# Layer 0's gated MLP: first projection as seven products of quarters, with weight sums on GpSimd

## The chip, the cores and the metric

One core of a Trainium2 chip runs the kernel. The metric is device time in microseconds (us) of one execution; runs are compared by their medians. Engines are TensorE (PE in the profile, with PEld for its weight loads), VectorE (DVE), ScalarE (ACT), GpSimd (POOL) and SyncE (SP), which issues the loads.

## The reference

A two-layer diffusion block over 512 latent tokens and 256 context tokens (768 together, `LAT` and `CTX`), model width 1024. Layer 0 mixes tokens with gated linear attention (GLA), layer 1 with neighbourhood attention. Behind each mixer stands a gated MLP, with a width-3 convolution along the tokens. With `h` the normalized and modulated input (`x * rms * (1 + scale) + shift`, where scale and shift come from adaLN projections of a condition vector), the MLP is

```python
a, v = jnp.split(h @ w_in, 2, axis=-1)            # 1024 -> 2 x 2816
a = conv3(a) + b                                  # per channel, along tokens; context and latent apart
x = x + gate * ((jax.nn.silu(a) * v) @ w_out)     # 2816 -> 1024
```

## The kernel before

Activations are kept with the channels on the 128 partitions and the tokens on the free axis. A number is split in a high and a low part (`hi`, `lo`); a product is three matmuls, `lo*hi`, `hi*lo`, `hi*hi` (`mm3`). Weights come from memory as 512 KB tiles `st` (128 x 1024, three buffers), issued by SP in order; ACT writes the high part `wh` (L244), DVE the low part `wl` (L245); five buffers hold each of them (`wunit`).

The hidden width 2816 is 22 tiles of 128 channels, in groups of three (the last of four). For each tile j, `in_tile` multiplies two weight tiles, `a` (the one that goes through the convolution) and the value `v`, with the eight channel blocks of `H`, for the 512 latent and the 256 context tokens: 2 x 8 x 3 matmuls of 512 columns and as many of 256. ACT copies the first result into `apad` (L788); DVE does the three taps (L822, L823, L824), ACT the silu (L825), DVE multiplies with the value out of PSUM (L830), and the result is split in `uh` and `ul` (L261, L262). After a group comes its output projection: for each of eight output blocks d, three tiles times LAT and CTX, added to the residual by DVE (`add_gated`, L273). The first two tiles (`in_first`) run over LAT while the normalization of CTX is being finished.

In layer 0's MLP, DVE also computes layer 1's adaLN vectors: `ada_lanes` gives 64 steps, each a 512 KB load `sa` and one multiply-add into `acc` (L203), four after each hidden tile.

Each engine runs its own queue in order. A scheduler decides that order from the dependencies and the buffers in the pools; only the program's own order and the pool sizes are written by hand.

Of the kernel before, what the change touches and what calls it, by code (L numbers as in the profile page):

```python
# [16 lines left out]
KD = 8  # L17
# [22 lines left out]
def body(ctx, tc, x, ctx_x, small, ada0, ada, w_gla, a_w1, a_w2, w_go, w_fi, w_fo,  # L40
# [8 lines left out]
    whl = ctx.enter_context(tc.tile_pool(name="whl", bufs=5))  # L49
# [49 lines left out]
    one0 = cst.tile([128, 32], F32, name="one0")  # L99
    nc.gpsimd.memset(one0, 0.0)  # L100
    nc.gpsimd.memset(one0[:, 0:1], 1.0)

# [61 lines left out]
    def ada_step(l, m, i):  # L164
# [12 lines left out]
        rows = sml.tile([128, 256], F32, name="rows", tag="rows", bufs=1)  # L177
# [10 lines left out]
    ada_jobs = []  # L188

    def ada_lanes(pool, l, m, c):  # L190
# [4 lines left out]
        def step(k):  # L195
            if k == 0:
                acc[0] = pool.tile([128, 1024], F32, name="acc", tag="acc", bufs=1)
# [9 lines left out]
            for j in range(4):  # L207
                mm(ps[32 * j:32 * j + 32, 0:256], one0, acc[0][:, 256 * j:256 * j + 256], start=True, stop=True,
                   skip_group_check=True)
            rows = sml.tile([128, 256], F32, name="rows", tag="rows", bufs=1)  # L210
            nc.scalar.activation(rows, ps[:, 0:256], AF.Copy)
            pm = ps_aux()
            for f in range(2):
                nc.tensor.transpose(pm[:, f * 128:(f + 1) * 128], rows[:, f * 128:(f + 1) * 128], ident)
            o = 8 * m
            mod = modT[l][:, o:o + 8, c]
            bias = sT[:, R_AB + 48 * l + o:R_AB + 48 * l + o + 8]
            nc.vector.tensor_add(mod.rearrange("p (j i) -> p j i", i=2),
                                 pm[:, 0:256].rearrange("p (i j s) -> p j i s", i=2, j=4)[:, :, :, 0],
                                 bias.rearrange("p (j i) -> p j i", i=2))  # L220
# [8 lines left out]

    def wunit(src, eng=None, scales=None):  # L230
# [3 lines left out]
        st = wst.tile([128, n], F32, name="st", tag="st")  # L234
        nc.sync.dma_start(st, src)
        hi = whl.tile([128, n], FR, name="wh", tag="wh")
        lo = whl.tile([128, n], FR, name="wl", tag="wl")
# [10 lines left out]
    def mm3(out, a, b, first, last):  # L248
        mm(out, a[1], b[0], start=first, stop=False)  # L249
        mm(out, a[0], b[1], start=False, stop=False)  # L250
        mm(out, a[0], b[0], start=False, stop=last)  # L251
# [23 lines left out]
    class Norm:  # L275


        def __init__(self, pool, l, n, rng, tag="t2", spread=False, blocks=False):
            self.__dict__.update(pool=pool, l=l, n=n, rng=rng, tag=tag, spread=spread, blocks=blocks)
            self.w = rng[1] - rng[0]  # L280
            self.acc = None

        def tmp(self, name):
            return self.pool.tile([128, 512], F32, name=name, tag=self.tag)[:, 0:self.w]

        def add(self, k):

            if self.acc is None:
                self.acc = self.pool.tile([128, self.w], F32, name="nacc", tag=f"nacc{self.w}", bufs=2)
# [24 lines left out]
        def apply(self, k):  # L314
# [5 lines left out]
            t = self.tmp("hf")  # L320
# [9 lines left out]
            nc.vector.scalar_tensor_tensor(lo, t, b_, hi.bitcast(F32), OP.add, OP.subtract)  # L330

# [38 lines left out]
    with tc.tile_pool(name="gla", bufs=6) as pool:  # L370
# [261 lines left out]
        def part_a(h, extra=None):  # L632
            vr_group(h, 0)
            diag(h)
            for i in range(7):
                level(h, i)
                todo = ada_step(*blocks.pop(0)) if blocks and i < 6 else None
# [93 lines left out]
    def finish_gla(pool):  # L731

        nonlocal X
        X = load_x()
        lat, cx = Norm(pool, 0, 1, LAT), Norm(pool, 0, 1, CTX)
        units = {}
        for d in range(KD):
            w, ps = early[d] if d < 3 else (out_unit(d), ps_mm())
# [16 lines left out]
    def ffn(l, after):  # L755
        first = 0 if l == 0 else 2
        seqs = ((0, 256), (256, 768)) if l == 0 else ((256, 768),)
        rngs = (LAT, CTX) if l == 0 else (LAT,)
        base = seqs[0][0]
        n_tok = 768 - base  # L760
        n_pad = n_tok + len(seqs) + 1

        def pad_of(tok):
            return tok - base + 1 + (1 if len(seqs) == 2 and tok >= 256 else 0)

        with tc.tile_pool(name=f"ffn{l}", bufs=4) as pool:
            left = finish_gla(pool) if l == 0 else []
            apad = [pool.tile([128, n_pad], F32, name=f"apad{i}", tag=f"apad{i}", bufs=1) for i in range(2)]
            edges = [0, n_pad - 1] + ([257] if len(seqs) == 2 else [])
            for ap_ in apad:  # L770
                for e in edges:
                    nc.gpsimd.memset(ap_[:, e:e + 1], 0.0)

            def pieces(a, b):
                return [(max(a, s0), min(b, s1)) for s0, s1 in seqs if max(a, s0) < min(b, s1)]

            def in_weights(j, which):
                return tuple(w.rearrange("p (k n) -> p k n", k=KD) for w in wunit(w_fi[l, j, which]))

            def in_group(j, which, w, rng):  # L780
                a, b = rng
                ps = ps_mm() if which == 0 else ps_aux()
                for k in range(KD):
                    mm3(ps[:, 0:b - a], (w[0][:, k, :], w[1][:, k, :]),
# [418 lines left out]
```

## Time and profile before

| what | value |
|---|---|
| median of three runs | 1739.43 us (1738.65 to 1744.02) |
| profiled execution | 1739.42 us, span 1737.6 us, mean granted clock 0.993 |
| TensorE busy | 1681.7 us, 97% |
| DVE, ACT, GpSimd busy | 1070.4 (62%), 658.7 (38%), 190.9 us (11%) |
| read from memory | 173.75 MB, 101 GB/s over the span |

Stages, in us from the span's start: first normalization and GLA 0 to 385; its output projection and second normalization to about 465; layer 0's MLP about 441 to 1040; neighbourhood attention 1050 to 1370; layer 1's MLP to the end. Rows of the profile give an instruction's start, duration, engine, line, operation, `out<-in` and shape; what stands in brackets is the idle time ahead of it and who ended that. Rows by form give the number of instructions, their busy time, the mean in ns and the idle time before them.

### The profile page before, as it was taken

The numbers are of one execution on the slowest core, as the hardware profiler recorded it, in microseconds if no ns is written. First come the engines' busy times: TensorE is split into PE (matmuls) and PEld (weight loads), VectorE is DVE, ScalarE is ACT, GpSimd is POOL, SyncE is SP. The second block draws the span as 40 slices with busy tenths as digits, with TensorE's granted clock in tenths as the row PEclk, the third lists the DMA queues.
The fourth block names the chain that finished last, engine by engine and source line by source line (L and its number), as shares of the span: only waits on it lengthen the run. The fifth ranks groups of instructions, "written<-read, shape, count | busy, mean of one in ns | idle before, by whom it ended". The sixth has DMA issues, their size and how long they took to land.

```text
span 1737.6 us, 27175 instructions
## 1 busy us (share of the span) xinstructions
PE 1681.7 (97%) x11107; PEld 1413.8 (81%) x11107; DVE 1070.4 (62%) x1699; ACT 658.7 (38%) x1173; POOL 190.9 (11%) x324
## 2 busy tenths in 40 slices
PE   5999999999999999999999999999999999999997
PEld 3767778778888888888888888888888888888887
DVE  4797777977666655656544575445456755555555
ACT  3675655653422121212213264443334522222332
POOL 1031212220000000000000015332222000000000
PEclk9999999999999999999999999999999999999999
DMA  7553423026224543544412122112111233223321
GB/s 274 173 171 122 154 90 104 19 72 220 86 73 152 160 125 110 179 147 146 122 60 86 49 68 79 54 42 66 54 56 42 75 97 98 90 82 95 109 85 49
DMA packets 54188, 179.70 MB, mean 103 GB/s; under 512 B 7024, under 2 KB 10864, under 8 KB 54064
## 3 DMA queue, kind: packets, MB, share of 16 engines
q1 hardware_dynamic: 54064, 177.97, 32.6%
q8 instruction: 87, 1.43, 0.3%
q14 instruction: 37, 0.30, 0.1%
HBM read 173.75 MB, written 2.10 MB: 101 GB/s over the span
## 4 chain that ended last, share of the span: by engine, by line
PE 80%; DVE 10%; ACT 4%; DMA 2%; issue 2%; POOL 1%; SPq 0%; POOLq 0%; DVEq 0%; ACTq 0%
PE mm L249 18%; PE mm L251 17%; PE mm L250 17%; PE aux L249 6%; PE aux L250 6%; PE aux L251 6%; PE mm L1006 2%; DMA sa<-in 2%; PE aux L989 2%; PE aux L964 2%; DVE t L526 1%; PE aux L605 1%; PE aux L570 1%; DVE acc L203 1%; DVE t L525 1%
## 5 line engine op out<-in xcount | busy, mean ns | idle before, releaser
L249 PE MATMUL mm<-hh,wl 128*128 128x512 f32 (+3 forms) x1104 | 388.6, 354 | 3.9 <-ACT hh L329 2.5
L251 PE MATMUL mm<-hh,wh 128*128 128x512 f32 (+3 forms) x1104 | 383.3, 348 | 0.0
L250 PE MATMUL mm<-hl,wh 128*128 128x512 f32 (+3 forms) x1104 | 383.0, 347 | 0.0
L244 ACT ACTIVATE wh<-st 128x1024 fp32r<-128x1024 f32 (+1 forms) x189 | 196.2, 1052 | 314.1 <-PE mm L251 162.4
L245 DVE TENSOR_TENSOR wl<-st,wh 128x1024 fp32r<-128x1024 f32 (+1 forms) x188 | 229.1, 1228 | 32.3 <-ACT wh L244 31.7
L249 PEld LDWEIGHTS mm<-hh,wl 128*128 128x128 f32 (+1 forms) x1104 | 208.8, 190 | 35.8 <-issue 5.5
L250 PEld LDWEIGHTS mm<-hl,wh 128*128 128x128 f32 (+1 forms) x1104 | 209.4, 190 | 24.3 <-issue 0.8
L251 PEld LDWEIGHTS mm<-hh,wh 128*128 128x128 f32 (+1 forms) x1104 | 209.1, 189 | 24.4 <-issue 0.4
L249 PE MATMUL aux<-hh,wl 128*128 128x512 f32 (+2 forms) x576 | 201.1, 349 | 0.0
L250 PE MATMUL aux<-hl,wh 128*128 128x512 f32 (+2 forms) x576 | 201.0, 349 | 0.0
L251 PE MATMUL aux<-hh,wh 128*128 128x512 f32 (+2 forms) x576 | 200.8, 349 | 0.0
L249 PE MATMUL mm<-uh,wl 128*128 128x512 f32 (+1 forms) x560 | 194.1, 350 | 1.7 <-ACT uh L261 1.4
L250 PE MATMUL mm<-ul,wh 128*128 128x512 f32 (+1 forms) x560 | 194.2, 348 | 0.0
L251 PE MATMUL mm<-uh,wh 128*128 128x512 f32 (+1 forms) x560 | 193.3, 346 | 0.0
L273 DVE SCALAR_TENSOR_TENSOR xl<-mm,mod,xl 128x512 f32<-128x512 f32 (+1 forms) x168 | 116.3, 698 | 108.9 <-PE mm L251 108.6
L305 POOL TENSOR_TENSOR rs<-ms,mhalf 128x2 f32<-128x2 f32 (+1 forms) x10 | 11.6, 1160 | 1036.6 <-DVE ms L303 1036.6
L249 PEld LDWEIGHTS mm<-uh,wl 128*128 128x128 f32 x560 | 105.8, 190 | 20.0 <-ACT uh L261 3.7
L249 PEld LDWEIGHTS aux<-hh,wl 128*128 128x128 f32 x576 | 109.2, 190 | 15.0 <-issue 1.4
L250 PEld LDWEIGHTS aux<-hl,wh 128*128 128x128 f32 x576 | 109.2, 190 | 14.4 <-issue 1.1
L251 PEld LDWEIGHTS aux<-hh,wh 128*128 128x128 f32 x576 | 109.1, 189 | 14.0 <-issue 0.8
L250 PEld LDWEIGHTS mm<-ul,wh 128*128 128x128 f32 x560 | 106.4, 190 | 14.3 <-DVE ul L262 0.3
L251 PEld LDWEIGHTS mm<-uh,wh 128*128 128x128 f32 x560 | 106.2, 190 | 13.1
(207 smaller groups left out, 2462.4 us busy)
## 6 DMA issues: line engine op xcount, KB each, us to landing
st<-in SPq DMA_DIRECT2D x201, 512.0 KB, 3.7
sa<-in SPq DMA_DIRECT2D x98, 512.0 KB, 4.3
sx<-in SPq DMA_DIRECT2D x14, 512.0 KB, 5.7
xl<-in SPq DMA_DIRECT2D x8, 512.0 KB, 5.6
xc<-in SPq DMA_DIRECT2D x4, 512.0 KB, 7.8
out<-y SPq DMA_DIRECT2D x16, 128.0 KB, 1.7
raw<-in SPq DMA_DIRECT2D x16, 96.0 KB, 2.4
t<-q SPq DMA_DIRECT2D x16, 64.0 KB, 2.0
```

The source lines that it names most:

```text
L203: nc.vector.scalar_tensor_tensor(acc[0], st, cs[:, k, c:c + 1], acc[0], OP.mult, OP.add)
L244: nc.scalar.activation(hi, st, AF.Copy)
L245: (eng or nc.vector).tensor_sub(lo, st, hi.bitcast(F32))
L249: mm(out, a[1], b[0], start=first, stop=False)
L250: mm(out, a[0], b[1], start=False, stop=False)
L251: mm(out, a[0], b[0], start=False, stop=last)
L273: nc.vector.scalar_tensor_tensor(x_, ps, gate(l, n, d, rng), x_, OP.mult, OP.add)
L525: nc.vector.tensor_mul(eq, eq, st[h]["q"])
L526: nc.vector.tensor_mul(ek, ek, st[h]["k"])
L964: mm(pss[hh][:, off:off + 256], qe[a_][p_, 128 * t:128 * t + 128], ke[b_][p_, ks], start=i == 0, stop=i == 2)
L989: nc.tensor.transpose(pT[:, i * 128:(i + 1) * 128], S2[:, o:o + 128], ident)
L1006: mm(po[64 * hh:64 * hh + 64, 128 * t:128 * t + 128], V[:, vs[i], 64 * hh:64 * hh + 64], PTs[hh][:, i * 128:(i + 1) * 128], start=i == 0, ...
```

## The change

`ffn` is written as `ffn0` and `ffn1`; layer 1's stays as it was. In layer 0, tiles 0 and 1 are computed as before (`plain`). For tiles 2 to 21 the product of the two weight tiles with `H` is seen as a 2 x 2 block product: output halves `a` and `v`, channel halves of four blocks, token halves of 384 columns. Eight quarter products become seven, by sums of weight quarters and of input quarters (the scheme of Strassen and Winograd):

- Input sums, once: GpSimd makes four sums for each of four block pairs out of `R` (the normalized input in full precision, which the normalization now writes as well, with one more ACT instruction a block). They are split into `T2`, `T3`, `T4`; quarter 12 of `H` is overwritten by a sum, the other three stay.
- Weight sums, per tile: GpSimd makes four sums of 128 x 512 in place (L928 to L931). `S1` goes to a buffer of its own, `S3` into the first half of the value tile, `S2` and `S4` into the halves of the first tile. Seven quarters are split by ACT (L237) and DVE (L238): `A` as one 1024-wide unit, the others 512 wide. The split parts go into a ring of ten 512-wide slots, in the order in which TensorE uses them.
- Order on TensorE per tile: `first` (products 11, 21), `middle` (2, 12, 3), `final_` (22, 4), 12 matmuls of 384 columns each; `first` of the next tile stands ahead of `final_` of this one, `middle` of the next behind it. Results are gathered in three PSUM buffers; ACT copies intermediate results out (`cp`, L867, three a tile) and DVE adds them (L948, L949, L959, L964).
- The middle tap of the convolution goes to ACT (L784). There is one `apad` instead of two.
- The output weights of a group come in halves of 512 columns, rearranged on the host beside the other layouts.
- adaLN: two steps a tile instead of four; the running sum takes one of the two `sa` buffers; half of the steps (m = 2 to 5) move into neighbourhood attention, four a pair of heads, of which the scheduler pulls some ahead. The end of a vector is eight matmuls of two columns instead of a product and transposes.

```diff
@@ ada_lanes
-                acc[0] = pool.tile([128, 1024], F32, name="acc", tag="acc", bufs=1)
+                acc[0] = ast.tile([128, 1024], F32, name="acc", tag="sa")
...
+            for d in range(KD):
+                mm(ps[:, 2 * d:2 * d + 2], acc[0][:, d * 128:d * 128 + 128], ones, start=True, stop=True)
@@ weights
+    NW = 10
+    WR = tuple(res.tile([128, NW * 512], FR, name=nm) for nm in ("wh", "wl"))
...
+    def wsplit(st):
+        out, o = [], 0
+        for a, b in wspans(st.shape[-1] // 512):
+            hi, lo = (w[:, a:b] for w in WR)
+            s_ = st[:, o:o + b - a]
+            nc.scalar.activation(hi, s_, AF.Copy)
+            nc.vector.tensor_sub(lo, s_, hi.bitcast(F32))
...
@@ Norm.apply
+            if self.keep:
+                nc.scalar.activation(t, t, AF.Identity, bias=b_)
@@ ffn0
+            def sums(k):
+                a, b = slice(0, HT), slice(HT, T)
+                r, q = R[k], R[k + 4]
+                sub = nc.gpsimd.tensor_sub
+                sub(r[:, a], r[:, b], r[:, a])
+                sub(r[:, b], q[:, b], r[:, b])
+                sub(q[:, b], q[:, b], r[:, a])
+                sub(q[:, a], q[:, a], q[:, b])
+                for i, src in ((2, q[:, b]), (3, r[:, b]), (4, q[:, a])):
+                    split_to(TT[i][0][:, k, :], TT[i][1][:, k, :], src)
...
+            def weights_b(j):
+                s_ = st[j]
+                a, v = s_["a"], wload(w_fi[0, j, 1])
+                s1 = pool.tile([128, 512], F32, name="s1", tag="s1")
+                h = (slice(0, 512), slice(512, 1024))
+                nc.gpsimd.tensor_add(s1, v[:, h[0]], v[:, h[1]])
+                nc.gpsimd.tensor_sub(v[:, h[0]], a[:, h[0]], v[:, h[0]])
+                nc.gpsimd.tensor_sub(a[:, h[0]], s1, a[:, h[0]])
+                nc.gpsimd.tensor_sub(a[:, h[1]], a[:, h[1]], a[:, h[0]])
+                for nm, t_ in (("S2", a[:, h[0]]), ("S1", s1), ("S3", v[:, h[0]])):
+                    s_[nm], = wsplit(t_)
+                s_["left"] = a[:, h[1]], v[:, h[1]]
...
+            def first(j):
+                s_["b1"], s_["b2"] = ps_aux(), ps_mm()
+                product(s_["b1"], s_["A"][0], 11, True)
+                s_["s1"] = copied(s_["b1"])
+                product(s_["b2"], s_["A"][1], 21, True)
...
+            def middle(j):
+                s_["b5"] = ps_aux()
+                product(s_["b1"], s_["S2"], 2, False)
+                s_["u2"] = copied(s_["b1"])
+                product(s_["b5"], s_["S1"], 12, True)
+                product(s_["b1"], s_["S3"], 3, False)
+                s_["u3"] = copied(s_["b1"])
+                nc.vector.tensor_add(s_["u3"], s_["b5"][:, 0:HT], s_["u3"])
+            def final_(j):
+                product(s_["b5"], s_["S4"], 22, False)
+                nc.vector.tensor_add(apad[:, 386:770], s_["b5"][:, 0:HT], s_["u2"])
+                product(s_["b1"], s_["A22"], 4, False)
+                u = finish(j, [(0, 256, b1[:, 0:256]), (256, HT, b1[:, 256:HT]), (HT, T, s_["u3"])])
+                for job in jobs[:2]:
+                    job()
...
+                    if j < NF - 1:
+                        weights_a(j + 1)
+                    weights_c(j)
+                    if j < NF - 1:
+                        first(j + 1)
+                    us[j] = final_(j)
+                    if j < NF - 1:
+                        to_pad(j + 1)
+                        weights_b(j + 1)
+                        middle(j + 1)
@@ neighbourhood attention, four times a pair of heads
+            jobs.pop(0)()
```

DVE in the second group, while a tile's hidden values are finished. Before, tile 4: `tt` is its convolution, `st` a weight tile, `sa` a load for adaLN.

```order
L822 TENSOR_SCALAR tt_5667<-apad0_4765,sT_109 128x769 [waits Activation_49]
L203 SCALAR_TENSOR_TENSOR acc_5679<-sa_5818,cs_115,acc_5679 128x1024 [waits DMAHW1_49,DVE_49]
L823 SCALAR_TENSOR_TENSOR tt_5667<-apad0_4765,sT_109,tt_5667 128x769 [waits DVE_49]
L245 TENSOR_TENSOR wl_5850<-st_5847,wh_5849 128x1024 [waits DMAHW4_49,PE_49,Activation_49]
L824 SCALAR_TENSOR_TENSOR tt_5667<-apad0_4765,sT_109,tt_5667 128x769 [waits DVE_49]
L203 SCALAR_TENSOR_TENSOR acc_5679<-sa_5821,cs_115,acc_5679 128x1024 [waits DMAHW2_49]
L830 TENSOR_TENSOR u_5672<-tt_5667,aux_5617 128x512 [waits PE_49,Activation_49]
L203 SCALAR_TENSOR_TENSOR acc_5679<-sa_5824,cs_115,acc_5679 128x1024 [waits DMAHW3_49,DVE_49]
L830 TENSOR_TENSOR u_5672<-tt_5667,aux_5642 128x256 [waits PE_49]
L245 TENSOR_TENSOR wl_5856<-st_5853,wh_5855 128x1024 [waits DMAHW5_49,Activation_49]
```

After, tiles 3 to 5: `tt_5514` is tile 3's convolution, `st_5589` and `st_5672` are tile 5's two weight tiles, `st_5727` is tile 6's first, and L948, L949 write tile 4's sum to `apad`.

```order
L238 TENSOR_TENSOR wl_121<-st_5589,wh_120 128x512 [waits Activation_49]
L786 SCALAR_TENSOR_TENSOR tt_5514<-apad_4166,sT_103,tt_5514 128x769 [waits DVE_49]
L238 TENSOR_TENSOR wl_121<-st_5672,wh_120 128x512 [waits DMAHW1_49,Activation_49]
L948 TENSOR_TENSOR apad_4166<-mm_5462,cp_5475 128x256 [waits DVE_49]
L949 TENSOR_TENSOR apad_4166<-mm_5462,cp_5475 128x128
L882 TENSOR_TENSOR tt_5514<-tt_5514,aux_5136 128x256 [waits PE_49,Activation_49]
L882 TENSOR_TENSOR tt_5514<-tt_5514,aux_5136 128x128
L882 TENSOR_TENSOR tt_5514<-tt_5514,cp_5262 128x384 [waits DVE_49]
L238 TENSOR_TENSOR wl_121<-st_5727,wh_120 128x1024 [waits DMAHW2_49,Activation_49]
L275 TENSOR_TENSOR ul_5520<-tt_5514,uh_5519 128x768 [waits Activation_49]
L959 TENSOR_TENSOR cp_5586<-aux_5547,cp_5586 128x384 [waits Activation_49]
L238 TENSOR_TENSOR wl_121<-st_5589,wh_120 128x512 [waits PE_49,Activation_49]
```

Between one tile's taps and products now stand the splits of a tile two further on, each behind ACT's high part, and three adds out of PSUM.

ACT at the same place. Before, tiles 4 and 5: `wh` the high parts of weights, `apad` the copies out of PSUM.

```order
L788 ACTIVATE apad0_4765<-mm_5559 128x512 [waits PE_49]
L788 ACTIVATE apad0_4765<-mm_5585 128x256 [waits PE_49]
L244 ACTIVATE wh_5849<-st_5847 128x1024 [waits DMAHW4_49,Activation_49]
L825 ACTIVATE tt_5667<-tt_5667 128x769 [waits DVE_49]
L244 ACTIVATE wh_5855<-st_5853 128x1024 [waits DMAHW5_49,PE_49,Activation_49]
L261 ACTIVATE uh_5675<-u_5672 128x768 [waits DVE_49]
L788 ACTIVATE apad1_4766<-mm_5698 128x512 [waits PE_49,Activation_49]
L788 ACTIVATE apad1_4766<-mm_5724 128x256 [waits PE_49,Activation_49]
```

After: `cp_5475`, `cp_5560` and `cp_5586` are tile 4's three copies, and the splits in between are of tile 5's sums (`s1_5674`, `st_5589`, `st_5672`) and of tile 6's first tile.

```order
L867 ACTIVATE cp_5475<-aux_5461 128x384 [waits PE_49]
L237 ACTIVATE wh_120<-st_5534 128x512 [waits DVE_49]
L237 ACTIVATE wh_120<-s1_5674 128x512 [waits PE_49,Pool_49]
L784 ACTIVATE tt_5514<-apad_4166,sT_103 128x769 [waits DVE_49]
L237 ACTIVATE wh_120<-st_5589 128x512 [waits Pool_49]
L237 ACTIVATE wh_120<-st_5672 128x512 [waits DMAHW1_49,PE_49]
L867 ACTIVATE cp_5560<-aux_5461 128x384 [waits PE_49]
L787 ACTIVATE tt_5514<-tt_5514 128x769 [waits DVE_49]
L237 ACTIVATE wh_120<-st_5727 128x1024 [waits DMAHW2_49,PE_49,Activation_49]
L274 ACTIVATE uh_5519<-tt_5514 128x768 [waits DVE_49,Activation_49]
L867 ACTIVATE cp_5586<-aux_5461 128x384 [waits PE_49]
```

Tile 4's second copy (`cp_5560`) now stands behind three splits that wait for GpSimd or a load; TensorE's third product of tile 4 waits for that copy.

GpSimd at the start of layer 0's MLP. Before, the edges of `apad` are cleared, and the next rows are reciprocal roots of normalizations.

```order
L772 MEMSET apad0_4765 128x1 [waits DMAHW3_49,DMAHW4_49,DMAHW2_49,DMAHW5_49,DMAHW1_49,DMAHW6_49,DMAHW0_49,DMAHW7_49,DVE_49,PE_49]
L772 MEMSET apad0_4765 128x1 x2
L772 MEMSET apad1_4766 128x1 x3
L257 TENSOR_TENSOR rs_4189<-ms_4187,mhalf_96 128x1 [waits Pool_49]
L305 TENSOR_TENSOR rs4_4484<-ms4_4482,mhalf_96 128x4 [waits DVE_49]
L305 TENSOR_TENSOR rs4_4806<-ms4_4804,mhalf_96 128x2 [waits DVE_49]
```

After, `s1_5073`, `st_5071` and `st_5037` belong to tile 2's weight sums, `R0` to `R7` to the input sums.

```order
L928 TENSOR_TENSOR s1_5073<-st_5071 128x512 [waits DMAHW0_49]
L929 TENSOR_TENSOR st_5071<-st_5037,st_5071 128x512 [waits DMAHW4_49,DMAHW5_49,DMAHW2_49,DMAHW7_49,Activation_49,Pool_49]
L930 TENSOR_TENSOR st_5037<-s1_5073,st_5037 128x512 [waits DMAHW3_49,DMAHW4_49,DMAHW1_49,DMAHW6_49,DVE_49,Pool_49]
L931 TENSOR_TENSOR st_5037<-st_5037 128x512 [waits Pool_49]
L846 TENSOR_TENSOR R0_4171<-R0_4171 128x384 [waits Activation_49]
L846 TENSOR_TENSOR R1_4172<-R1_4172 128x384 [waits Activation_49]
L847 TENSOR_TENSOR R0_4171<-R4_4167,R0_4171 128x384 [waits Pool_49]
L847 TENSOR_TENSOR R1_4172<-R5_4168,R1_4172 128x384 [waits Pool_49]
L848 TENSOR_TENSOR R4_4167<-R4_4167,R0_4171 128x384 [waits Pool_49]
L848 TENSOR_TENSOR R5_4168<-R5_4168,R1_4172 128x384 [waits Pool_49]
```

Tile 2's four weight sums and then sixteen input sums (the first of them in the rows shown) stand in GpSimd's queue, which had nothing there.

More of the change, by code (lines that the diff above doesn't have):

```diff
@@ L206, in step @@
             ps = ps_aux()
[L207 to L214, printed above, removed]
+            for d in range(KD):
+                mm(ps[:, 2 * d:2 * d + 2], acc[0][:, d * 128:d * 128 + 128], ones, start=True, stop=True)
             o = 8 * m
             mod = modT[l][:, o:o + 8, c]
[L217 to L220, printed above, removed]
+            nc.vector.tensor_add(mod, ps[:, 0:16:2], sT[:, R_AB + 48 * l + o:R_AB + 48 * l + o + 8])
             if m in (1, 4):
@@ L246, in wunit, with mm3 @@
         return hi, lo
[L248 to L251, printed above, removed]
+    def mm3(out, a, b, first, last, **at):
+        mm(out, a[1], b[0], start=first, stop=False, **at)
+        mm(out, a[0], b[1], start=False, stop=False, **at)
+        mm(out, a[0], b[0], start=False, stop=last, **at)
     def rstd_of(ss, n):
@@ L752, in finish_gla @@
         return todo + cx.steps()
[L755 to L769, printed above, removed]
+    GROUPS = [tuple(range(3 * g, 3 * g + 3)) for g in range(6)] + [(18, 19, 20, 21)]
@@ L770, in ffn, with ffn1 @@
+    def ffn1(after):
+        n_tok = N_LAT
+        with tc.tile_pool(name="ffn1", bufs=4) as pool:
+            apad = [pool.tile([128, n_tok + 2], F32, name=f"apad{i}", tag=f"apad{i}", bufs=1) for i in range(2)]
             for ap_ in apad:
[L771 removed]
+                for e in (0, n_tok + 1):
                     nc.gpsimd.memset(ap_[:, e:e + 1], 0.0)
[L774 to L775 removed]
```

309 lines of the change are left out of this document (215 added, 94 removed).

## The prediction

> **What bounds the kernel now.** I read the busy shares first, then the chain that ended last, then busy time by stage (span, busy PE, PEld, DVE, ACT, POOL, clock, DMA share, GB/s).
>
> ```profile
> PE 1681.7 (97%) x11107; PEld 1413.8 (81%) x11107; DVE 1070.4 (62%) x1699; ACT 658.7 (38%) x1173; POOL 190.9 (11%) x324
> PE 80%; DVE 10%; ACT 4%; DMA 2%; issue 2%; POOL 1%; SPq 0%; POOLq 0%; DVEq 0%; ACTq 0%
> 505.00:582.00 77.00, 77.00 (x454) 67.08 (x453) 44.83 (x55) 17.35 (x23) 0.00 (x0) 1.00 0.38 123
> 893.00:970.00 77.00, 77.00 (x443) 68.00 (x442) 32.97 (x41) 17.29 (x22) 0.00 (x0) 1.00 0.20 62
> 1050.00:1370.00 320.00, 314.88 (x2345) 265.98 (x2344) 173.57 (x401) 132.93 (x284) 92.76 (x185) 0.99 0.18 54
> ```
>
> Layer 0's MLP lies at about 441 to 1040 us. In it TensorE never rests, DVE is 43 to 58% busy in the two windows shown, GpSimd does nothing. So TensorE's matmuls set the time there, and fewer of them is a real gain as long as the work that moves to DVE, ACT and GpSimd stays hidden. Whether it does is the whole question.
>
> The boundaries are read from TensorE's rows (start, duration):
>
> ```profile
> 913.16 0.40 PE L249 MATMUL mm<-hh,wl 128*128 128x512 f32 x1
> 929.84 0.40 PE L249 MATMUL mm<-hh,wl 128*128 128x512 f32 x1
> 484.23 0.40 PE L249 MATMUL mm<-hh,wl 128*128 128x512 f32 x1
> 526.23 0.40 PE L249 MATMUL mm<-hh,wl 128*128 128x512 f32 x1
> 67.84 0.33 PE L249 MATMUL aux<-hh,wl 128*128 128x384 f32 x1
> 68.71 0.34 PE L251 MATMUL aux<-hh,wh 128*128 128x384 f32 x1
> ```
>
> The first two are the starts of tile 18 and tile 19: a hidden tile takes 16.68 us. The next two are the starts of tile 2 and tile 3, with tile 2 and an output projection between: 42.00 − 16.68 = 25.3 us for that projection. From tile 3's start to tile 18's, five groups take 386.9 us, 77.4 each. The last two rows bound five steps of 384-column matmuls: 0.174 us each.
>
> **The change, part by part.**
>
> *TensorE.* Tiles 2 to 21 go from 96 matmuls (16.68 us) to 84 of 384 columns: 84 × 0.174 = 14.6 us. That is −2.1 us × 20 = −41 us if nothing waits. The output projection keeps its matmuls.
>
> *What each tile adds.* Durations by form:
>
> ```profile
> L245 DVE TENSOR_TENSOR wl<-st,wh 128x1024 fp32r<-128x1024 f32 x187 | 228.4, 1231 | 32.3 <-ACT wh L244 31.7
> L262 DVE TENSOR_TENSOR ul<-u,uh 128x512 fp32r<-128x512 f32 x22 | 15.1, 685 | 1.4 <-ACT uh L261 1.4
> L262 DVE TENSOR_TENSOR hl<-aux,hh 128x384 fp32r<-128x384 f32 x12 | 6.0, 546 | 0.0
> L823 DVE SCALAR_TENSOR_TENSOR tt<-apad,sT,tt 128x769 f32<-128x769 f32 x22 | 22.4, 1020 | 0.6
> L203 DVE SCALAR_TENSOR_TENSOR acc<-sa,cs,acc 128x1024 f32<-128x1024 f32 x56 | 71.8, 1282 | 29.4 <-DMA sa<-in 29.3
> L261 ACT ACTIVATE uh<-u 128x512 fp32r<-128x512 f32 x22 | 13.6, 617 | 2.8 <-DVE u L830 2.8
> L261 ACT ACTIVATE hh<-aux 128x384 fp32r<-128x384 f32 x12 | 5.2, 508 | 1.3 <-PE aux L618 1.3
> st<-in SPq DMA_DIRECT2D x201, 512.0 KB, 3.7
> sa<-in SPq DMA_DIRECT2D x98, 512.0 KB, 4.3
> ```
>
> DVE's splits go from 2 × 1.23 = 2.5 to 1.23 + 5 × 0.685 = 4.7 us, plus four adds out of PSUM (about 1.9), minus the first convolution tap (0.7, moved to ACT): about +3.4 us a tile. ACT gets three copies (1.5), more split instructions (+1.6) and the tap (0.85). Both engines have room on average; what matters is the order they stand in. The bytes loaded stay the same. Of the two adaLN load buffers one now holds the running sum, so each of those steps waits for a load behind the step before, 4.3 + 1.3 = 5.6 us apart; two a tile fit in 14.6 us: 0. SP issues all loads in one order; an adaLN load ahead of a weight load waits for nothing longer than that.
>
> *GpSimd.* It gets four 512-column sums a tile, and before the first product of the scheme 16 sums of 384. No row shows that size, so I bound it by the nearest ones:
>
> ```profile
> 285.83 0.72 POOL L594 TENSOR_TENSOR xl<-xl,er 128x256 f32<-128x256 f32 x1
> 30.43 2.63 POOL L245 TENSOR_TENSOR wl<-st,wh 128x1024 fp32r<-128x1024 f32 x1 [9.36 <-ACT wh L244]
> 30.75 2.85 DVE L328 SCALAR_TENSOR_TENSOR hf<-xl,modA,rb 128x512 f32<-128x512 f32 x1
> L328 DVE SCALAR_TENSOR_TENSOR hf<-xl,modA,aux 128x512 f32<-128x512 f32 x8 | 6.0, 748 | 2.2 <-PE aux L308 2.2
> 115.63 4.81 POOL L594 TENSOR_TENSOR xl<-xl,er 128x256 f32<-128x256 f32 x1 [3.90 <-ACT er L593]
> 119.77 0.38 DVE L535 COPY_PREDICATED attd<-lvl,aux 128x192 f32<-128x192 uint8 x1
> ```
>
> Half of 2.63, and twice 0.72, give 1.3 to 1.4 us for a 512-column sum, 1.0 for 384. That is the low end. The other rows show the high end: DVE's two-operand instruction took 2.85 us instead of 0.75 because GpSimd was reading, and ended 0.5 us after GpSimd did; GpSimd's 0.72 us sum took 4.81 us and ended 0.67 us after DVE came to an instruction that reads PSUM. So a GpSimd sum and a DVE instruction with two operands in SBUF do not run together, and a DVE that has such instructions ready can shut GpSimd out for several of them. The Trainium skill ("SBUF — State Buffer", section "Who interferes with whom") says that such a DVE instruction contends with a GpSimd instruction that reads SBUF, over a port pair held exclusively for the whole instruction. It reads as a turn for each; by that a sum would wait for one DVE instruction at most, three sums for 3 us in the worst case. The first row pair agrees with it, the 4.81 us shows that more than one may pass. DVE's two-operand work per tile is 1.23 + 4 × 0.685 + 0.685 + 2 × 1.02 + 0.95 (768-column split) = 7.7 us of 14.6, so on average half of GpSimd's sums meet it. I take 1 to 3 us per tile for the lock.
>
> *The loop that this closes.* Three load buffers now hold the weights through the sums. The value weights of tile K+1 can be loaded only when DVE has split the last sum of tile K (it lies in tile K's first buffer); the splits of the sums of K+1 stand in ACT's queue ahead of a copy out of PSUM which the next product waits for. So round the loop: issue and load 4.0 (3.7 to 4.3 by the rows), three sums 3 × 1.3 = 3.9, two 512-column splits on ACT 1.2, copy 0.5, the third product's 12 matmuls 2.1, copy 0.5, DVE's add 0.55, DVE's split 0.7: 13.5 us, and eight handovers at about 0.1 us make 14.3. TensorE's tile is 14.6 us, so without the lock the loop just fits; with 1 to 3 us of lock TensorE waits about 0.7, 3.4 and 2.4 us in the three tiles of a group (the first is fed by what was prepared during the output projection). Three tiles take 3 × 14.6 + 6.5 = 50.3, with the projection's 25.3 behind them 75.6 us a group, against 77.4. In two of the five groups five or six steps of the adaLN sums (1.28 us each, two SBUF operands) stand between the tiles' own DVE work instead of beside the output projection; of these 7 us I count 4.6 on the loop: 80.2. Five groups: 3 × 75.6 + 2 × 80.2 = 387 against 386.9: nothing gained. Without the lock, with 1.3 us of small waits a group, 3 × 70.4 + 2 × 75 = 361: −26.
>
> *The first group.* Here nothing hides the new work:
>
> ```profile
> 464.05 0.48 DVE L330 SCALAR_TENSOR_TENSOR hl<-hf,mod,hh 128x256 fp32r<-128x256 f32 x1 [0.58 <-ACT hh L329]
> ```
>
> The normalized input is complete at about 464.5, the extra ACT writes add about 1. GpSimd then has 4 × 1.3 + 16 × 1.0 = 21 us, to 486.5; with 16 DVE splits of 0.55 that it must share with, about 491. TensorE ends the two plain tiles at 484.2 and tile 2's first two products at 488.4. The scheme's order on TensorE is products 11 and 21, then 2, 12 and 3, then 22 and 4, of 2.1 us each. After tile 2's products 2 and 12, product 3 needs the copy that stands in ACT's queue behind the splits of tile 3's sums: DVE's split frees the buffer (491.7), the load lands at 496, four sums to 502 or so, three ACT splits and one 768-column write 2.7, copy 0.5, handovers: about 507. TensorE idles some 4 us and 12 us. From 507: 2.1 (product 3) + 4.2 (rest of tile 2) + 10.4 (tile 3's first five products) + 25.3 = 549, where tile 3's start was at 526.2: +23. The ends are 534 (no wait: 484.2 + 14.6 + 10.4 + 25.3, +8) and 554 (the four sums at twice their time). Without the lock the first wait goes and the sums take 5 instead of 6 us: 543, +17.
>
> *The last group* has 10.4 us of its four tiles already done: 4 × 14.6 − 10.4 = 48 us, plus some 8.5 of waits 56.5, against 68.4 before (four tiles and 1.7): −12; without the lock 51, −17.
>
> *The neighbourhood-attention stage* gets 32 adaLN steps (of which some eight move forward into the MLP's last output phase), up to 32 × 1.28 = 41 us of DVE where 147 of 320 us are free, so mostly hidden; but softmax waits for DVE there. Ends 0 and +10; I take +3. The GLA stage gives up nothing; 16 extra ACT writes and the later start of the first product cost 2. Eight two-column matmuls instead of transposes for each adaLN end: 0.
>
> *Sum* against the profiled execution's 1739.42 us (the median is 1739.43): first group +23, five groups 0, last group −12, start and attention +5: +16, 1755 us.
>
> **Rivals.**
> (a) The lock costs little because DVE, in order, stops by itself for PSUM and for GpSimd's results and so lets the sums through. Then +17 − 26 − 17 + 5 = −21: 1718 us. My sum moves from −21 to +16 as the lock goes from 0 to 2 us a tile, so this decides below about 0.9 us a tile: for it speak DVE's 43% and the 0.72 us row; against it the 4.81 and 2.85 us rows.
> (b) Everything is hidden, the first group too: TensorE's −41 alone, 1698. Against it: the loop of 14.3 us leaves nothing over.
> (c) Half the lock, by the same line 0.9 to 1.4 us a tile: within 5 us of no change.
> (d) Waits cost the clock as well. In the trace the granted clock is lower where TensorE pauses:
>
> ```profile
> 425.00:430.00 5.00, 4.15 (x24) 3.95 (x24) 2.23 (x4) 0.85 (x2) 1.45 (x1) 0.72 0.39 111
> 1000.00:1015.00 15.00, 14.17 (x98) 13.57 (x97) 8.61 (x18) 6.70 (x12) 1.01 (x1) 0.89 0.00 1
> ```
>
> In the second, pauses of 0.8 us in all stand beside a clock of 0.89: 1.6 us of lost speed in 15. With some 40 waits of 2 to 3 us, a third of them followed by 1 to 2 us at reduced speed, +15 to +25 on my sum: 1775. How long a wait has to be for that, these rows don't tell. The Trainium skill ("TensorE: Matmul & The Clock Gate", section "HAM oscillation — how this bites in real kernels") describes such a gate; its figures enter nowhere here.
>
> **Chances.** From no change 0.3% (5.2 us) is about what can be told apart. The locked loop, with or without lost clock: 0.50 (of this 0.14 for (d)); (c) 0.14; (a) 0.28; (b) 0.08. So faster 0.36, same 0.14, slower 0.50. The range leaves out (b) and the worst of (d): 1714 to 1776. The locked case's own range is 1745 to 1776.
>
> **What the profile after would show.** Right: between 485 and 550 us two TensorE waits of together 12 to 18 us, for ACT's copy or DVE's split; in each group TensorE's busy share below 95%, with waits named ACT or DVE; GpSimd sums of 1.3 us alone and 2 to 5 beside DVE; DVE two-operand instructions of 2 us and more; a group period of about 75 to 80 us. Wrong: GpSimd sums all near 1.3 us and a group period near 70 us (a); no wait in 485 to 550 (b); a clock under 0.95 throughout 500 to 1040 (d). The sum is most easily spoiled by the loop's load and sums being prepared a tile earlier than I read from the queues, which would hide them, and by the first group, whose 23 us is a hand-made schedule.

## The result and the profile after

The changed kernel takes 1753.64 us (median; 1752.43 to 1758.08) against 1740.74 for the kernel before on the same chip (one run more than the three of the table before): 1.0073 times as long, 95% interval 1.005 to 1.0096. Its profiled span is 1752.0 us against 1737.6, +14.4.

The page after, busy shares and chain:

```profile
PE 1663.9 (95%) x10915; PEld 1428.2 (82%) x10915; DVE 1179.3 (67%) x1877; ACT 735.5 (42%) x1323; POOL 341.0 (19%) x415
PE 58%; DVE 19%; DMA 10%; ACT 5%; issue 4%; POOL 4%; SPq 0%; POOLq 0%; DVEq 0%; ACTq 0%
```

TensorE has 17.8 us less to do, and its share of the chain falls from 80% to 58%: DVE (19%) and loads (10%) have taken its place. By stage, in the columns of the prediction's windows:

```profile
505.00:582.00 77.00, 74.53 (x424) 70.61 (x423) 49.00 (x70) 27.07 (x42) 17.32 (x12) 1.00 0.19 62
893.00:970.00 77.00, 73.56 (x406) 69.00 (x406) 59.56 (x82) 27.28 (x42) 18.93 (x12) 0.98 0.39 129
1050.00:1370.00 320.00, 312.12 (x2317) 262.48 (x2316) 189.02 (x399) 126.33 (x268) 97.42 (x181) 0.99 0.29 90
```

TensorE, without a gap before in the first two stretches, now rests 2.5 and 3.4 us of 77; DVE is 4 and 27 us busier; GpSimd has 17 to 19 us. To see where the 14.4 us arise, the same places of the program are laid side by side (before: L249 and L1006, after: L262 and L1201): tile 2's first product, the starts behind the first and the sixth output projection, layer 1's last latent projection, and the first and last values products of the attention.

```profile
487.55 0.34 PE L262 MATMUL aux<-hh,wl 128*128 128x384 f32 x1
547.09 0.34 PE L262 MATMUL aux<-hh,wl 128*128 128x384 f32 x1
924.20 0.34 PE L262 MATMUL aux<-hh,wl 128*128 128x384 f32 x1
1044.04 0.40 PE L262 MATMUL mm<-hh,wl 128*128 128x512 f32 x1
1059.31 0.88 PE L1201 MATMUL mm<-PT,V 128*64 128x128 f32 x12
1339.91 0.33 PE L1201 MATMUL mm<-PT,V 128*64 128x128 f32 x2
```

```profile
1044.32 0.40 PE L249 MATMUL mm<-hh,wl 128*128 128x512 f32 x1
1059.57 0.66 PE L1006 MATMUL mm<-PT,V 128*64 128x128 f32 x8
1327.79 1.09 PE L1006 MATMUL mm<-PT,V 128*64 128x128 f32 x16
```

With 484.23, 526.23 and 913.16 of before (in the prediction), the changed kernel is 3.3 us behind at tile 2, 20.9 behind the first group, 11.0 behind at the last, 0.3 *ahead* where the attention begins, and 12.1 behind at its end. So the MLP as a whole gained and lost nothing, and the attention, whose matmuls the change did not touch, lost the time.

In the MLP the matmuls did get shorter; TensorE's list of waits between 440 and 1060 us shows what took that back (its largest entry, and two at the output projections):

```profile
PE aux L262 <- ACT cp L867: 23.5, 11, 3.7
PE mm L262 <- ACT uh L274: 1.2, 2, 0.8
PE mm L263 <- DVE ul L275: 1.1, 2, 0.6
```

One of the waits in order of time, in the third group (start, duration); counted from the tile whose taps (L785, L786) DVE does here, the copy and the product are of the next tile, the sums and splits of the one after it:

```profile
630.25 1.30 POOL L928 TENSOR_TENSOR s<-st 128x512 f32<-128x512 f32 x1 [22.34 <-DMA st<-in]
630.31 2.04 DVE L785 SCALAR_TENSOR_TENSOR tt<-apad,sT,tt 128x769 f32<-128x769 f32 x1 [1.10 <-ACT tt L784]
631.62 1.88 POOL L929 TENSOR_TENSOR st<-st 128x512 f32<-128x512 f32 x1
632.28 1.77 DVE L238 TENSOR_TENSOR wl<-s,wh 128x512 fp32r<-128x512 f32 x1
633.58 1.59 POOL L930 TENSOR_TENSOR st<-s,st 128x512 f32<-128x512 f32 x1
633.97 2.02 DVE L786 SCALAR_TENSOR_TENSOR tt<-apad,sT,tt 128x769 f32<-128x769 f32 x1
635.20 1.15 ACT L237 ACTIVATE wh<-st 128x512 fp32r<-128x512 f32 x2 [2.99 <-POOL st L930]
636.26 0.47 ACT L867 ACTIVATE cp<-aux 128x384 f32<-128x384 f32 x1
636.78 0.69 PE L262 MATMUL aux<-T3h,wl 128*128 128x384 f32 x1 [3.33 <-ACT cp L867]
```

DVE's taps take 2.0 us (1.02 before), its 512-column split 1.77 (0.69), while GpSimd's sums take 1.6 to 1.9 instead of 1.3. They go in turns: each ends a step after the other's. ACT waits for the third sum, splits twice, and only then makes the copy for which TensorE has stood still since about 633.4.

### The profile page after: what moved, and what is told of

The parts are those of the page before. It is cut to its first block, busy times and chain, and to the rows that moved or that the text cites. A ratio compares the mean times of both kernels' runs of the same rounds, so it can differ in the third digit from the quotient of the medians.

```text
span 1752.0 us, 27282 instructions
## 1 busy us (share of the span) xinstructions
PE 1663.9 (95%) x10915; PEld 1428.2 (82%) x10915; DVE 1179.3 (67%) x1877; ACT 735.5 (42%) x1323; POOL 341.0 (19%) x415
## 4 chain that ended last, share of the span: by engine, by line
PE 58%; DVE 19%; DMA 10%; ACT 5%; issue 4%; POOL 4%; SPq 0%; POOLq 0%; DVEq 0%; ACTq 0%
PE mm L262 13%; PE mm L264 13%; PE mm L263 13%; DMA sa<-in 6%; DMA st<-in 4%; PE aux L262 4%; PE aux L264 3%; PE aux L263 3%; DVE wl L238 3%; DVE acc L196 2%; PE mm L1201 2%; PE aux L1184 1%; DVE tt L785 1%; PE aux L1159 1%; DVE tt L786 1%
## 5 line engine op out<-in xcount | busy, mean ns | idle before, releaser
L262 PE MATMUL mm<-hh,wl 128*128 128x512 f32 (+3 forms) x864 | 307.5, 358 | 4.8 <-ACT hh L346 2.5
L263 PE MATMUL mm<-hl,wh 128*128 128x512 f32 (+3 forms) x864 | 302.1, 350 | 0.1
L264 PE MATMUL mm<-hh,wh 128*128 128x512 f32 (+3 forms) x864 | 301.9, 350 | 0.0
L262 PE MATMUL mm<-uh,wl 128*128 128x512 f32 (+1 forms) x544 | 189.8, 349 | 1.2 <-ACT uh L274 1.2
L262 PEld LDWEIGHTS mm<-hh,wl 128*128 128x128 f32 (+1 forms) x864 | 162.9, 189 | 28.8 <-issue 5.4
L262 PE MATMUL aux<-hh,wl 128*128 128x384 f32 (+2 forms) x496 | 174.8, 353 | 0.5 <-DVE cp L959 0.2
L264 PE MATMUL aux<-hh,wh 128*128 128x384 f32 (+2 forms) x496 | 173.8, 350 | 0.0
L263 PE MATMUL aux<-hl,wh 128*128 128x384 f32 (+2 forms) x496 | 173.8, 350 | 0.0
L237 ACT ACTIVATE wh<-st 128x512 fp32r<-128x512 f32 (+1 forms) x126 | 92.4, 753 | 186.4 <-PE mm L264 108.9
L258 DVE TENSOR_TENSOR wl<-st,wh 128x1024 fp32r<-128x1024 f32 (+1 forms) x126 | 153.8, 1227 | 23.2 <-ACT wh L257 22.8
L238 DVE TENSOR_TENSOR wl<-st,wh 128x512 fp32r<-128x512 f32 (+1 forms) x126 | 116.0, 935 | 31.2 <-ACT wh L237 25.9
L262 PEld LDWEIGHTS mm<-uh,wl 128*128 128x128 f32 x544 | 102.3, 188 | 18.5 <-ACT uh L274 3.8
L196 DVE SCALAR_TENSOR_TENSOR acc<-sa,cs,acc 128x1024 f32<-128x1024 f32 x56 | 74.7, 1334 | 42.0 <-DMA sa<-in 41.5
```

Source lines behind the costliest of these rows:

```text
L196: nc.vector.scalar_tensor_tensor(acc[0], st, cs[:, k, c:c + 1], acc[0], OP.mult, OP.add)
L237: nc.scalar.activation(hi, s_, AF.Copy)
L238: nc.vector.tensor_sub(lo, s_, hi.bitcast(F32))
L258: (eng or nc.vector).tensor_sub(lo, st, hi.bitcast(F32))
L262: mm(out, a[1], b[0], start=first, stop=False, **at)
L263: mm(out, a[0], b[1], start=False, stop=False, **at)
```

## The experiments

Each was timed beside runs of the kernel before on its own chip; ratios are to those. Numbers in the expectations are against the changed kernel's 1753.6 us.

**Sums replaced by clears of the same length.**

```diff
-                nc.gpsimd.tensor_add(s1, v[:, h[0]], v[:, h[1]])
...
+                for t_ in (s1, v[:, h[0]], a[:, h[0]], a[:, h[1]]):
+                    for _ in range(3):
+                        nc.gpsimd.memset(t_, 0.0)
```

> The four weight sums of a tile are left out; in their place GpSimd clears the same four 512-column pieces three times each (write only, by the 768-column clears of the profile about 0.47 us each, so 1.4 us a piece, as long as a sum). The product of weights is then not the reference's. Theory A (shared port): a GpSimd sum and a DVE instruction with two operands in SBUF shut each other out, and that lengthens the loop; without GpSimd reads DVE's taps return from 1.56 to about 1.02 us, its 512-column splits from 0.81 to 0.69, TensorE's waits on ACT's copy (24 us) fall by more than half: 1753.6 - 20 = 1734 us, within 6. Rival B (length alone): load, sums and splits are simply too long a chain, lock or not; DVE gets faster but the waits stay: 1750 to 1755 us.

Measured: 1724.2 us, ratio 0.9901 (0.9886 to 0.9916). GpSimd is as busy as with the sums (339.5 against 341.0 us), its clears 0.527 us each, 1.58 a piece. By form, in the changed kernel and then in this one:

```profile
L238 DVE TENSOR_TENSOR wl<-st,wh 128x512 fp32r<-128x512 f32 x88 | 70.1, 811 | 9.8 <-ACT wh L237 9.8
L785 DVE SCALAR_TENSOR_TENSOR tt<-apad,sT,tt 128x769 f32<-128x769 f32 x22 | 34.3, 1560 | 8.8 <-ACT tt L784 8.8
L786 DVE SCALAR_TENSOR_TENSOR tt<-apad,sT,tt 128x769 f32<-128x769 f32 x22 | 27.1, 1234 | 0.1
L238 DVE TENSOR_TENSOR wl<-s,wh 128x512 fp32r<-128x512 f32 x20 | 22.3, 1114 | 18.6 <-ACT wh L237 18.6
L931 POOL TENSOR_TENSOR st<-st 128x512 f32<-128x512 f32 x20 | 32.9, 1646 | 1.6
```

```profile
L238 DVE TENSOR_TENSOR wl<-st,wh 128x512 fp32r<-128x512 f32 x88 | 59.9, 687 | 24.8 <-ACT wh L237 24.7
L785 DVE SCALAR_TENSOR_TENSOR tt<-apad,sT,tt 128x769 f32<-128x769 f32 x22 | 22.4, 1020 | 10.7 <-ACT tt L784 10.7
L786 DVE SCALAR_TENSOR_TENSOR tt<-apad,sT,tt 128x769 f32<-128x769 f32 x22 | 22.4, 1018 | 0.5
L238 DVE TENSOR_TENSOR wl<-s,wh 128x512 fp32r<-128x512 f32 x20 | 13.7, 687 | 1.1
```

and its list of TensorE's waits:

```profile
PE aux L262 <- ACT cp L867: 3.4, 1, 3.4
```

Every one of these DVE forms is back at its length of before, and TensorE's wait on the copy falls from 23.5 to 3.4 us (one wait, before tile 2's first T product, where the input sums still run on GpSimd). The gain, 29 us, is larger than theory A expected. The DVE rows show the contention. Whether length plays a part as well the run doesn't tell, because a clear reads nothing and so doesn't wait as a sum does. Of a tile's twelve clears on GpSimd nine run before its value weights have landed, in this tile those of `s1` and of its first weight tile; only the three of the value tile wait for the load:

```profile
549.84 1.70 POOL L930 MEMSET s<- 128x512 f32 x3
557.58 2.87 POOL L930 MEMSET st<- 128x512 f32 x6 [6.04 <-DVE wl L238]
562.37 1.70 POOL L930 MEMSET st<- 128x512 f32 x3 [1.93 <-DMA st<-in]
```

So the chain from the load to the splits is shorter here too, 1.7 us in place of four sums; the next run bears on that.

What the DVE rows show is the contention of the page "SBUF — State Buffer" of the Trainium skill (section "Who interferes with whom"): a DVE instruction with two SBUF operands against a GpSimd instruction that reads SBUF, not against one that only writes it. This pair of runs agrees on both halves. From the four DVE rows in the change and in this run, 88 × 0.124 + 22 × 0.54 + 22 × 0.218 + 20 × 0.427 = 36 us over 20 tiles: DVE lost 1.8 us a tile.

**Sums on DVE.** `nc.gpsimd` becomes `nc.vector` in the four lines.

> The four weight sums run on DVE in place of GpSimd (nothing left out). DVE gets 4 x 0.685 = 2.7 us more a tile and loses the 1.8 us a tile by which its instructions are longer now. Theory A: the sums take 2.1 instead of 4.6 us in the loop and block nothing; TensorE's waits fall by half: about 1740 us, within 7. Rival B: DVE's queue becomes the loop, its sums stand behind taps and splits; 1750 us or more.

Measured: 1722.91 us, ratio 0.9895 (0.9877 to 0.9913). More than expected; it is as good as the clears. This run answers the rival of length. The first and the third sum of one tile in the changed kernel, on GpSimd, and then of the same tile here, on DVE:

```profile
570.09 1.29 POOL L928 TENSOR_TENSOR s<-st 128x512 f32<-128x512 f32 x1 [10.52 <-DMA st<-in]
572.84 1.62 POOL L930 TENSOR_TENSOR st<-s,st 128x512 f32<-128x512 f32 x1
```

```profile
565.83 0.69 DVE L928 TENSOR_TENSOR s<-st 128x512 f32<-128x512 f32 x1 [2.50 <-DMA st<-in]
569.14 0.69 DVE L930 TENSOR_TENSOR st<-s,st 128x512 f32<-128x512 f32 x1
```

A sum is shorter on DVE, but DVE's other instructions stand between the sums: from the first one's start to the third one's end it is 4.0 us here (in nine of the 20 tiles, and more in six), as much as three sums of 1.29 us take on GpSimd one behind the other. With contention that stretch is 4.4 us in this tile, and 4.0 to 5.1 over the tiles. So a chain as long as GpSimd's own sums does not make TensorE wait, and the rival of length alone falls. How TensorE's waits divide between the longer sums, DVE's longer instructions and the later loads behind them is not measured. The time is also that of leaving the sums out:

**No sums.** The four lines are deleted and S1 is split from `v[:, h[1]]`.

> The four weight sums of a tile are left out altogether, S1 to S4 are split from unsummed halves, so the result is not the reference's. It gives the whole price of the sums, lock and length together. Theories A and B both: TensorE's waits on ACT's copy nearly vanish, the first group's too: -30 us, 1724, within 8. If it stays over 1745, the sums were not what TensorE waited for, and the splits or loads were.

Measured: 1725.03 us, ratio 0.9904 (0.9888 to 0.9919). With the contention gone, doing the sums on DVE costs nothing that shows. In the run with the sums on DVE:

```profile
L931 DVE TENSOR_TENSOR st<-st 128x512 f32<-128x512 f32 x20 | 13.7, 685 | 0.1
540.00:610.00 70.00, 70.00 (x409) 66.97 (x408) 54.23 (x87) 26.66 (x41) 0.00 (x0) 1.00 0.32 98
```

A sum takes 0.685 us on DVE against 1.3 to 1.6 in the mean on GpSimd, and in this stretch TensorE is busy without a gap again, with DVE at 77%.

**A bank of its own for product 3.**

```diff
-                product(s_["b1"], s_["S3"], 3, False)
-                s_["u3"] = copied(s_["b1"])
-                nc.vector.tensor_add(s_["u3"], s_["b5"][:, 0:HT], s_["u3"])
+                s_["b3"] = ps_mm()
+                product(s_["b3"], s_["S3"], 3, True)
+                s_["u3"] = pool.tile([128, HT], F32, name="cp", tag="cp", bufs=3)
+                nc.vector.tensor_add(s_["u3"], s_["b5"][:, 0:HT], s_["u2"])
+                nc.vector.tensor_add(s_["u3"], s_["b3"][:, 0:HT], s_["u3"])
...
-                product(s_["b1"], s_["A22"], 4, False)
-                b1 = s_["b1"]
+                product(s_["b3"], s_["A22"], 4, False)
+                b1 = s_["u2"]
+                nc.vector.tensor_add(b1, s_["b3"][:, 0:HT], b1)
```

> Product 3 goes to a PSUM bank of its own and is added by DVE afterwards, so TensorE needn't wait for ACT's second copy; ACT's third copy is left out, DVE gets one 384-column add more (0.55 us a tile). Sums stay on GpSimd. Theory A/B as told (TensorE waits because the copy stands behind the next tile's splits in ACT's queue): the 24 us on the copy go, and few others come: 1753.6 - 20 = 1733 us, within 7. Rival C (supply): the splits themselves are late, so the wait only changes its name, to the split of S3 or the first tap: 1748 us or more.

Measured: 1766.34 us, ratio 1.0142 (1.0127 to 1.0157), slower than the change by some 12 us. The wait changed its name:

```profile
PE aux L262 <- DVE cp L960: 13.5, 6, 4.4
PE mm L262 <- ACT uh L274: 7.0, 4, 2.8
PE aux L262 <- ACT cp L867: 3.7, 1, 3.7
```

My expectation fell, and the time is on rival C's side, though the waits are on DVE's adds rather than on the split or the tap that it named. The edit does more than the expectation says: product 4 goes into the new bank as well, and DVE gets two adds of 384 columns a tile instead of one, 2 × 0.55 us, on the engine that the contention slows. So what the copy alone is worth stays open.

**The attention without its adaLN steps.** The four `jobs.pop(0)()` are deleted; constants stand for the vectors m = 2 to 5.

> The changed kernel without the 32 adaLN steps (m = 2 to 5) that it moved into neighbourhood attention; they are left out altogether and constants stand in their place. Reading of the two traces: at the first values product of the attention both kernels are level (1059.6 and 1059.3 us), at the last ones the changed kernel is 12 us behind, so the steps cost 12 us there and about 2 more: 1753.6 - 13 = 1740.5 us, within 3, level with before. Rival: the attention is late for another reason (its queues are ordered anew), and 1748 us or more remain.

Measured: 1737.06 us, ratio 0.999 (0.998 to 0.9999): all of the 0.73% is gone, and the reading of the traces held. With the steps there, only 24 of the 32 stand in the attention; the scheduler had pulled the first vector's eight to 894 to 931 us, in the MLP, and left its end at 1111 us.

**Without the vectors' ends.** Seven of the eight matmuls that end each of these vectors are left out.

> The changed kernel with the 32 steps in place, but of the eight two-column matmuls that end each of those four vectors only one is done. If TensorE pays for the matmuls themselves (1.7 us a vector in its rows): -4 x 1.5 = -6, 1747.5 us, within 2; the rest of the 13 us is then DVE's time. If they run in gaps: 1753 us.

Measured: 1748.24 us, ratio 1.0056 (1.0041 to 1.0071), against 1.0073 for the change: 3 us by the ratios, whose intervals overlap, 5 by the medians; about what was expected if TensorE pays for the matmuls. The traces say more: from its first to its last values product the attention takes 268.2 us before, 280.6 with the change, 274.2 in this run and 268.3 without the steps. So of some 14 us 3 to 6 are the ends; the rest goes with the steps on DVE.

**All steps back in the MLP, weight sums on DVE.** `jobs[:4]` a tile, eight vectors, none in the attention.

> Nothing left out: weight sums on DVE as in the run before, and all 64 adaLN steps back in layer 0's MLP, four a tile, none in the attention. Theory: attention gives back 13 us; the MLP takes four vector ends of 1.7 us and 32 DVE steps that mostly fit beside the output projections: 1722.9 - 13 + 7 + 2 = 1719 us, within 5. Rival: DVE, now with the sums, has no room for 64 steps in the MLP (32 x 1.28 = 41 us more on its queue): 1728 us or more.

Measured: 1723.11 us, ratio 0.9917 (0.9899 to 0.9935): no difference from 1722.9 with half of them in the attention. What the attention gives back the MLP takes; TensorE's waits on the copy rise from 4.3 to 7.5 us there, and the ends cost TensorE as much as elsewhere. With the sums on DVE, moving these steps was neutral as such; they cost much the same on either side.

**Input sums on DVE too.** `sub = nc.vector.tensor_sub`, on top of the weight sums.

> Nothing left out: weight sums and the sixteen input sums on DVE. Sixteen sums on GpSimd take about 1.0 us each alone and block DVE's splits beside them; on DVE they are 16 x 0.55 = 8.8 us and block nothing. TensorE's wait before the first T2 product (3.7 us, on ACT's first copy) then goes: 1722.9 - 4 = 1719 us, within 3. Rival: DVE's queue holds everything at that place, the wait stays or grows: 1723 us or more.

Measured: 1715.78 us, ratio 0.9868 (0.9852 to 0.9885). A little more than expected. The wait before the first T2 product is gone, the first output projection ends at 536.4 instead of 544.6.

**Only the input sums on DVE.**

> The changed kernel with the sixteen input sums on DVE and the weight sums still on GpSimd; nothing left out. It parts the 38 us between the changed kernel and the run with both on DVE. If the two prices add up: the first group's part is the 7 us between the runs with weight sums on DVE, 1753.6 - 7 = 1746.5 us, within 3, and the loop keeps its waits. If the first group's wait only goes over into the loop behind it: 1752 us or more.

Measured: 1752.11 us, ratio 1.0077 (1.005 to 1.0104), no difference from the change. Behind the first group this kernel is 4.2 us ahead of it (542.85 against 547.09), at the last group 1.8 (922.44 against 924.20). The time is the rival's, but the waits did not grow: between these two places TensorE rests 16.2 us in this run and 16.4 in the change. What differs is the pace of its matmuls. Here three waits, of 2.91, 2.58 and 1.97 us, were followed by ten or so matmuls 0.32 us apart instead of 0.174, in the change only one was; two more such stretches, at about 1.5 us each, cover the 2.5 us lost. After the shortest of them:

```profile
876.37 0.44 PE L262 MATMUL aux<-T3h,wl 128*128 128x384 f32 x1 [1.97 <-ACT cp L867]
877.38 0.53 PE L263 MATMUL aux<-T3l,wh 128*128 128x384 f32 x1
877.70 0.53 PE L264 MATMUL aux<-T3h,wh 128*128 128x384 f32 x1
```

**Two load buffers in the attention.** The running sum gets a tile in the attention's pool.

> All sums on DVE, nothing left out, and in neighbourhood attention the running adaLN sum lies in a buffer of its own, so that two loads can be under way instead of one. In the changed kernel DVE waits 19.3 us there for those loads, with softmax instructions behind it. If these waits are what the attention lost: 1715.8 - 5 = 1711 us, within 3. If it is DVE's own 32 x 1.28 us and the vectors' ends: 1715 us or more.

Measured: 1727.74 us, ratio 0.9937 (0.9915 to 0.9959): 12 us worse than without it. DVE's wait on the loads between 990 and 1380 us did fall. In the kernel with all sums on DVE and one load buffer:

```profile
DVE acc L196 <- DMA sa<-in: 22.6, 18, 5.3
```

and in this one:

```profile
DVE acc L198 <- DMA sa<-in: 6.4, 3, 3.5
```

But the attention from its third values product to its last took 266.5 us against 266.1. So those waits cost nothing that shows. The eight steps that had run at 860 to 909 us could not be pulled ahead any more, since their tile exists only once the MLP's pool is free: they ran at 1003 to 1028, beside the normalization, and 10 us were lost between the last group and the attention's third values product. Another 4 us were lost before the first projection's end; I have no cause for these, and the profiled execution, 1732.0 us, is itself 4 us above the median.

**All sums on DVE and all steps in the MLP.**

> All sums on DVE and all 64 adaLN steps back in layer 0's MLP; nothing left out. With only the weight sums on DVE that placement cost as much in the MLP as it gave back in the attention (1723.1 against 1722.9). With the first group free of waits it should be the same: 1716 us, within 4. If DVE's room in the MLP was what cost it: 1711 us or less is not expected, 1722 or more would be the sums' queue filling up.

Measured: 1715.44 us, ratio 0.9866 (0.9842 to 0.9889), level with 1715.78. These two are the fastest that compute the whole block, 1.3% below the kernel before; with only the weight sums on DVE it was 1%.

## Why the prediction was right, and where not

The direction and the sum (+16 forecast, +12.9 measured by the medians, +14.4 by the spans) came out, the terms did not all, and the total owes something to luck:

| term | forecast | measured |
|---|---|---|
| first group, with the later start | +23 (and part of +2) | +20.9 |
| five groups | 0 | −9.8 |
| last group, up to the attention | −12 | −11.3 |
| attention and after | +3 | +14.7 |

*The loop.* The mechanism was right, as the 630 to 637 us of the trace and the run with the sums on DVE show: ACT's second copy stands behind the splits of the next tile's sums, and those are late because GpSimd and DVE shut each other out. Its price a tile, 1 to 3 us, was meant for the sums and was too high there: three of them take 4.0 to 5.1 us in the loop, 0 to 1.1 more than alone. The rest of the price was DVE's, whose own instructions lost 1.8 us a tile. What failed is the step from there to TensorE: "0.7, 3.4 and 2.4 us in the three tiles of a group". Behind the first group the trace has waits on the copy of 1.5 to 3.3 us, as large as drawn, but one or two a group: 13.4 us over the five groups, where I had 32. They took 73.6 to 76.6 us each, instead of 75.6 to 80. The extra 4.6 us for groups with adaLN steps did not show.

Against this the sum left something out. In the run with all sums on DVE, where TensorE never waits between the same places, the five groups take 354.4 us, not the 345.5 of 5 × (3 × 14.6 + 25.3): a group in which an adaLN vector ends takes 1.8 us more for its products than one in which none does (45.85 against 44.10), and four of the five have one. So the loop cost 377.1 − 354.4 = 22.7 us, rests and slower matmuls behind them, where 32 + 9 were drawn.

*The first group* was nearly right in size, with smaller waits than drawn (3.7, 2.0 and 1.0 us in place of 4 and 12), and a start 3.3 us late in place of 2.

*The attention* is the mis-sized term: "mostly hidden", +3. I had divided DVE's idle time by the work; that softmax waits in the same queue in order I had named, and priced too low. The run without the steps puts the price at about 14 us, the ends 3 to 6 of it. The prediction's "Eight two-column matmuls instead of transposes for each adaLN end: 0" looked at how an end is done, and missed where, and what it takes: 1.84 us of TensorE an end in its rows.

The two errors, −10 and +12, cancelled. That is luck: the forecast was better than its working. Of the signs it named, DVE instructions of 2 us and groups of about 74 to 77 us came; GpSimd's sums beside DVE took up to 2.4 us, not 2 to 5, and the two waits of together 12 to 18 us were three of 6.7.

*The rivals.* (a) expected 1718 us with hardly any contention; the clears, without it, give 1724, with the attention's 14 in it. So the MLP itself was worth more than I gave it: with the sums on DVE the attention's third values product comes 31 us earlier than before (1045.7 against 1076.7), with half of the adaLN steps moved out. (b), everything hidden, 1698 us, no run reached: with all sums on DVE and hardly a wait left it is 1716, and TensorE's busy time is 29.5 us below that of before, not 41. (c), half the lock and no change, is what the MLP by itself came to (−0.3 us at the attention's start). (d) was real but small: matmuls after the longest waits ran slowly,

```profile
637.27 0.52 PE L263 MATMUL aux<-T3l,wh 128*128 128x384 f32 x1
639.51 0.52 PE L264 MATMUL aux<-T3h,wh 128*128 128x384 f32 x1
640.08 0.34 PE L263 MATMUL aux<-T3l,wh 128*128 128x384 f32 x1
```

0.32 us a matmul instead of 0.174 for about 3 us, at a granted clock of 0.50, after 3.33 us of rest; in this trace the matmuls after a wait of 2.47 us (at 729.5) came 0.18 apart. Three such places in the MLP cost some 4 us.

## What to carry to other kernels

Work is not free because its engine is idle: GpSimd's weight sums cost 30 us here, while the same sums cost nothing that shows on DVE, which was already the busier engine. Look at the durations of the neighbour's instructions, not only at the waits: they show contention directly. A clear of the same length in place of the suspected instruction keeps its engine busy but drops its dependencies, so it doesn't by itself tell contention from latency; the same work on another engine, with the length of the chain read from the trace, did. And where steps move to another stage, count what each costs there in the queue it enters: an engine's idle share says little if what it idles between is waited for.

## What the runs showed of the hardware that I had not expected

GpSimd and DVE went mostly in turns here (sums of 1.3 to 2.4 us, no 4.8 us as in the row of before), and it was DVE that lost more: 36 us against 18 for GpSimd's 80 sums (1.51 us in the mean against 1.29). A rest of TensorE can nearly halve its pace for about 3 us, but the length of the rest alone doesn't decide it: in the changed kernel's MLP rests of 3.2 to 3.7 us did and those of 2.5 and 2.7 did not, while with only the input sums on DVE rests of 2.0 and 2.6 us did and those of 2.4 and 2.5 did not.
